# LayerNorm of all tokens beside the last expert unit, and a ring of 20 weight tiles, in a trunk layer with a hierarchical mixture of experts

## The chip, the cores and the metric

The kernel runs on one core of a Trainium2 chip. The metric is the device time of one execution in microseconds (us). The kernel before was timed in three runs.

## What is computed

One layer of a decoder trunk over 1024 tokens of width 1024, in float32. Token mixing (a Conformer convolution and a Mamba-2 scan side by side, and an output projection) ends in the first LayerNorm; each token then goes through two of 64 experts, and a second LayerNorm closes the layer. The change lies in the second half:

```python
x = layer_norm(DEEPNORM_ALPHA * x + g1 * mix, ln1_g[l], ln1_b[l])
h = x * (1.0 + sc2) + sh2
ffn = hier_moe(h, ...)              # each token: 2 experts of the 8 in its best group
x = layer_norm(DEEPNORM_ALPHA * x + g2 * ffn, ln2_g[l], ln2_b[l])
...
def expert_block(args):             # w1, w3: 1024 x 512, w2: 512 x 1024
    xb, e = args
    return (jax.nn.silu(xb @ w1[e]) * (xb @ w3[e])) @ w2[e]
```

## The kernel before, in words

Up to about 1080 us it does the token mixing; that part is the same in both kernels but for two instructions. Eight tiles of 128 tokens come out of the first LayerNorm; each is written to DRAM twice, as `x1d` (the normed token, L1003) and as `h2d` (modulated, what the experts read). The router's result is turned into tables of token numbers, gates and row numbers (`gidx`, `gslot`, `ridx`).

**The expert stage.** Every expert has six weight loads of 1 MB (w1, w3 and w2 in two halves each), so the plan has 64 x 6 = 384 loads. They go through a ring of 14 SBUF tiles (`N_RING`), all issued on the queue of SyncE (SP) by `load` (L244), in the order of the plan. A load is issued when the load that had its tile 14 places earlier has been used by every product that needs it (`emitted`). The first 13 (`N_EARLY`) are issued before the routing is known to the end, by a guess of the expert numbers (`fix_i`); the others follow the row `fix_l`, which is written behind the second gather.

Experts are ranked by their number of tokens, and 28 letters (`ORDER`) say how they are put together into units of at most 128 tokens: F and L are units of two experts, S of four, H of one, T is three units for two heavy experts (t4, t4x, t5 and so on; all three use the same weights). For experts of the small ranks the load is conditional: an expert without tokens is not read. The last unit is `s60`, the four smallest.

A unit (`unit`) gathers its tokens' rows from `h2d` into `xg` by an indirect DMA of GpSimd (POOL), transposes them on TensorE (`tp`), multiplies with w1 and w3 (`h0`, `h1`, L1325), takes Silu on ScalarE and the product on VectorE (`s1`), transposes (`th`), multiplies with w2 (`yp`, L1344), scales by the gate (L1349, VectorE) and scatters the rows into `ybuf` by another indirect DMA (L1283, POOL). `ybuf` has two rows per token, one for each of its experts. All the scatters write the same DRAM tensor and go one behind the other's landing.

**The end of before.** `load_sums` (L1270) reads `x1d` back into an SBUF tile `acc` of 4 MB at the start of the expert stage, and ScalarE multiplies it by alpha. `collect` (L1279, L1280) stands inside the last unit: 16 times it loads half of a tile's `ybuf` rows (0.5 MB, through two buffers `yb`) on POOL's queue and adds it into `acc` on VectorE. The last unit scatters nothing: its rows are split into a high and a low part and added by products with 0/1 matrices (`hots`, L1550) in `finish`, on top of `acc` (a product with the identity, L1541). `finish` then does the second LayerNorm tile by tile (L1551 to L1575) and stores on SP's queue (L1576). A loop for the tokens of overfull experts follows.

Of the kernel before, what the change touches and what calls it, by code (L numbers as in the profile page):

```python
# [19 lines left out]
P = 128  # L20
# [12 lines left out]
N_RING = 14  # L33
N_RING_A = 8
N_EARLY = 13
# [26 lines left out]
HW = 8  # L62
N_PRE = 3
# [7 lines left out]
FIN = "AV,VA,VA,VA,VA,VA,VA,VV".split(",")  # L71
# [24 lines left out]
ORDER = "FFSLSTLSHHLSTLSHHLSHHLHHSLLS"  # L96
# [5 lines left out]
def trunk(ctx: ExitStack, tc: tile.TileContext, x, c, w_ada, b_ada, w_in, conf_conv_w, conf_conv_b,  # L102
# [159 lines left out]
    with ExitStack() as p1:  # L262
# [64 lines left out]
        def ada_late(r, rows):  # L327
# [10 lines left out]
            else:  # L338
# [9 lines left out]
                nc.gpsimd.tensor_tensor(sc2_bc, sc2_bc, l1g_bc, op=OP.mult)  # L348

# [824 lines left out]
    with ExitStack() as p2:  # L1174
# [41 lines left out]
        rows = acc[:, 0, :].bitcast(BF16).rearrange("p (j t) -> p j t", t=P)  # L1216
# [42 lines left out]
    with ExitStack() as p3:  # L1259
# [8 lines left out]
        def load_sums():  # L1268
            for i in range(8):
                nc.scalar.dma_start(acc[:, i, :], x1d[i * P:(i + 1) * P, :])  # L1270
            for i in range(8):
                nc.scalar.activation(acc[:, i, :], acc[:, i, :], AF.Copy, scale=ALPHA)

        def collect():

            for i in range(8):
                for k in range(2):
                    yb = wk.tile([P, D], F32, tag="yb", bufs=2, name=f"yb{i}_{k}")
                    nc.gpsimd.dma_start(yb, ybuf[2 * i * P:2 * (i + 1) * P, :].rearrange("(t k) d -> t k d", k=2)[:, k, :])  # L1279
                    nc.vector.tensor_tensor(acc[:, i, :], acc[:, i, :], yb, op=OP.add)  # L1280

# [3 lines left out]
        load_sums()  # L1285
# [17 lines left out]
        def unit(nm, ws, cols, last=False):  # L1303
# [4 lines left out]
            if last:  # L1308
                collect()
# [20 lines left out]
            nc.scalar.activation(s1, hps[0], AF.Silu)  # L1330
            nc.vector.tensor_tensor(s1, s1, hps[1], op=OP.mult)  # L1331
# [18 lines left out]
            if not last:  # L1350
                send_rows(y, rcol)
                return

            trel = wk.tile([P, 8], F32, tag="trel", bufs=2, name=f"trel{nm}")
            nc.vector.tensor_scalar(trel, toff, -1.0, tcol, op0=OP.mult, op1=OP.add)
            hots = []
            for j in range(0, 8, HW):
                hot = wk.tile([P, HW, P], F32R, tag="hot", bufs=1, name=f"hot{nm}_{j}")
                nc.vector.tensor_tensor(hot, jf[:, None, :].to_broadcast([P, HW, P]),
                                        trel[:, j:j + HW, None].to_broadcast([P, HW, P]), op=OP.is_equal)  # L1360
                hots += [hot[:, i, :] for i in range(HW)]
            ys = []
            for n in range(2):
                yh, yl = (wk.tile([P, 512], F32R, tag=f"y{p_}", bufs=2, name=f"y{p_}{nm}_{n}") for p_ in "hl")
                nc.scalar.copy(yh, y[:, half[n]])
                nc.vector.tensor_tensor(yl, y[:, half[n]], yh, op=OP.subtract)
                ys.append((yh, yl))
            return hots, ys, y, rcol
# [95 lines left out]
        def emitted():  # L1464

            while sent[0] < len(plan):
                n = sent[0]
                if n >= N_RING and uses[n - N_RING] > 0:
                    break
                r, which, hf = plan[n]  # L1470
                if n >= min(N_RING, 6 * N_FIX):
                    load(ring[n % N_RING], *place_regs(r), which, hf)
# [11 lines left out]
        def tiles(r):  # L1484
            def of(which, hf):
# [3 lines left out]
                return ring[n % N_RING]  # L1489
# [30 lines left out]
        assert list(first.values()) == [P_TRI, P_HVY, P_LGT, P_SML, NE]  # L1520
        emitted()
# [6 lines left out]
        spare = [ring[(len(plan) + j) % N_RING] for j in range(N_RING)]  # L1528
        l2g_bc, l2b_bc = spare[0][:, 0:D], spare[0][:, D:2 * D]
        outs = [spare[1 + i // 2][:, D * (i % 2):D * (i % 2) + D] for i in range(8)]  # L1530
        banks = [("z", "z"), ("h0", "h1"), ("tp", "tp"), ("yp", "yp")] * 2

        def finish(nm, hots, ys, pre):

            zp = {}

            def z_open(i):
                zp[i] = [ps.tile([P, 512], F32, tag=banks[i][n], bufs=bufs_of[banks[i][n]], name=f"z{nm}{i}_{n}")
                         for n in range(2)]
                for n in range(2):  # L1540
                    nc.tensor.matmul(zp[i][n], ident, acc[:, i, half[n]], start=True, stop=not ys)  # L1541
            for i in range(pre):
                z_open(i)
            for i in range(8):
                if i >= pre:
                    z_open(i)
                bs = wk.tile([P, 2, 6], F32, tag="bs", bufs=4, name=f"bs{nm}{i}")
                for n in range(2):
                    for j in range(2 if ys else 0):
                        nc.tensor.matmul(zp[i][n], hots[i], ys[n][j], start=False, stop=(j == 1))  # L1550
                    nc.vector.bn_stats(bs[:, n, :], zp[i][n])  # L1551
                mv = wk.tile([P, 2], F32, tag="mv", bufs=4, name=f"mv{nm}{i}")
                nc.vector.bn_aggr(mv, bs)
                rs = wk.tile([P, 1], F32, tag="rs", bufs=4, name=f"rs{nm}{i}")
                nc.scalar.activation(rs, mv[:, 1:2], AF.Sqrt, bias=eps)
                nc.vector.reciprocal(rs, rs)
                t_ = outs[i]
                if "A" in FIN[i]:
                    nm_ = wk.tile([P, 1], F32, tag="nm", bufs=4, name=f"nm{nm}{i}")
                    nc.vector.scalar_tensor_tensor(nm_, mv[:, 0:1], -1.0, rs, op0=OP.mult, op1=OP.mult)  # L1560
                for n in range(2):
                    if FIN[i][n] == "V":

                        nc.vector.scalar_tensor_tensor(t_[:, half[n]], zp[i][n], mv[:, 0:1], l2g_bc[:, half[n]],
                                                       op0=OP.subtract, op1=OP.mult)
                    else:
# [61 lines left out]
```

## Time and profile before

| | |
|---|---|
| three runs | 2156.46, 2159.21, 2159.33 us |
| median | 2159.21 us |
| the profiled execution | 2157.99 us |
| its span, first to last instruction | 2156.0 us |
| mean granted TensorE clock | 0.94 |
| busy share of the span | TensorE 85%, VectorE 50%, GpSimd 29%, ScalarE 25% |
| expert stage | from about 1080 us to the end |

The profiled execution's own time lies 2.0 us above its span and 1.2 us below the median. The busy shares are means over the whole span: VectorE's 50% comes nearly all from the token mixing, and in the expert stage TensorE and the DMA engines carry the work.

### The profile page before, as it was taken

How to read it: one execution, taken by the hardware profiler on the slowest of the kernel's cores; microseconds unless marked ns; L12 is line 12 of the kernel's file. 1: busy time of each engine (PE TensorE's matmuls, PEld its weight loads, DVE VectorE, ACT ScalarE, POOL GpSimd, SP SyncE). 2: the span in 40 equal slices, each digit the busy share in tenths (PEclk: the TensorE clock that was granted, in tenths of full speed). 3: DMA queues.
4: the chain of work that ended last, by engine and by line, in shares of the span. 5: the costliest groups of instructions: out<-in, count | busy, mean ns of one | idle time of the engine just before them, and what ended most of it. 6: DMA issues, size and time to landing. Idle time of an engine off the chain costs nothing.

```text
span 2156.0 us, 23640 instructions
## 1 busy us (share of the span) xinstructions
PE 1826.5 (85%) x8135; PEld 1012.6 (47%) x8135; DVE 1073.0 (50%) x1796; ACT 547.7 (25%) x990; POOL 619.1 (29%) x440
## 2 busy tenths in 40 slices
PE   4897989689989999889678969989799897998784
PEld 1365656558667767767432313324234241433232
DVE  1499898977999999897830301000000000000036
ACT  0234535264344446443320000001000010000011
POOL 0345656651544346553510000100001000000014
PEclk7998999889989999999879999999999998999997
DMA  8877877646443425657489999899998999999964
GB/s 260 288 256 240 249 252 232 230 145 219 153 131 132 165 93 171 206 182 279 171 312 419 419 421 383 339 420 420 419 374 338 420 420 420 420 409 372 420 255 160
DMA packets 204278, 626.01 MB, mean 290 GB/s; under 512 B 25566, under 2 KB 91350, under 8 KB 157308
## 3 DMA queue, kind: packets, MB, share of 16 engines
q1 hardware_dynamic: 156080, 552.79, 66.9%
q10 hardware_dynamic: 36700, 46.51, 6.7%
q0 software_dynamic: 11376, 25.18, 3.3%
q8 instruction: 65, 1.06, 0.2%
q14 instruction: 57, 0.47, 0.1%
HBM read 576.08 MB, written 83.44 MB: 306 GB/s over the span
## 4 chain that ended last, share of the span: by engine, by line
PE 30%; DMA 26%; DVE 20%; issue 4%; ACT 2%; POOL 1%; ACTq 0%; SPq 0%; DVEq 0%; POOLq 0%
DMA ring<-in_expert_w_dram 24%; DVE acc L620 8%; PE mix L475 5%; PE h0h L1325 2%; PE h1h L1325 2%; PE ypl L1344 2%; PE yph L1344 2%; PE ypt L1344 1%; PE h1l L1325 1%; PE h0t L1325 1%; PE px L475 1%; PE h1t L1325 1%; PE h0l L1325 1%; DVE cy L694 1%; DVE ctl L950 1%
## 5 line engine op out<-in xcount | busy, mean ns | idle before, releaser
L620 DVE SCALAR_TENSOR_TENSOR acc<-u,cw,acc 128x512 f32<-128x512 f32 x426 | 433.3, 1029 | 17.5 <-ACT acc L609 13.5
L1290 POOL DMA_INDIRECT xg<-h2d,gidx x32 | 33.0, 1033 | 724.0 <-PE tph L1298 203.8
L475 PE MATMUL px<-hTh,wx_hl 128*128 128x512 f32 x512 | 175.3, 413 | 3.5 <-ACT wx_hl L448 3.0
L475 PE MATMUL mix<-wo_hl,cth 128*128 128x512 f32 x416 | 136.2, 421 | 14.9 <-DVE wo_hl L449 10.2
L1325 PE MATMUL h1s<-ring,xTs 128*32 128x512 f32 x512 | 99.3, 691 | 42.6 <-DMA ring<-in_expert_w_dram 42.6
L1344 PE MATMUL yps<-ring,hTs 128*32 128x512 f32 x512 | 109.5, 599 | 19.3 <-DMA ring<-in_expert_w_dram 16.9
L1331 DVE TENSOR_TENSOR s1s<-s1s,h1s 128x512 f32<-128x512 f32 x8 | 5.5, 688 | 223.2 <-PE h1s L1325 223.2
L475 PEld LDWEIGHTS px<-hTh,wx_hl 128*128 128x128 f32 x512 | 99.0, 195 | 36.0 <-ACT wx_hl L448 5.2
L475 PE MATMUL px<-hTl,wx_hl 128*128 128x512 f32 x256 | 105.1, 410 | 0.0
L475 PEld LDWEIGHTS mix<-wo_hl,cth 128*128 128x128 f32 x416 | 81.1, 199 | 38.4 <-DVE wo_hl L449 14.1
L449 POOL TENSOR_TENSOR wo_hl<-wo,wo_hl 128x512 fp32r<-128x512 f32 x52 | 76.1, 1473 | 60.5 <-ACT wo_hl L448 60.1
L305 PE MATMUL ada<-wada,cond 128*32 128x512 f32 x192 | 74.2, 673 | 21.9 <-DMA wada<-in_w_ada_dram 21.8
L475 PE MATMUL pg<-hTh,wg_hl 128*128 128x512 f32 x256 | 90.1, 419 | 1.9 <-ACT wg_hl L448 0.9
L1325 PE MATMUL h0s<-ring,xTs 128*32 128x512 f32 x512 | 75.6, 639 | 16.3 <-DMA ring<-in_expert_w_dram 16.3
L475 PE MATMUL pz<-hTh,wz_hl 128*128 128x512 f32 x256 | 86.2, 404 | 2.1 <-ACT wz_hl L448 1.1
L475 PE MATMUL mix<-wo_hl,ctl 128*128 128x512 f32 x208 | 80.3, 422 | 7.4 <-DVE ctl L950 7.3
L475 PE MATMUL pv<-hTh,wv_hl 128*128 128x512 f32 x256 | 85.7, 405 | 0.4 <-DVE h L514 0.4
L1325 PEld LDWEIGHTS h1s<-ring,xTs 128*32 128x32 f32 x512 | 22.0, 124 | 116.1 <-DMA ring<-in_expert_w_dram 75.3
L1349 DVE SCALAR_TENSOR_TENSOR ys<-yps,gslot,g_bc 128x512 f32<-128x512 f32 x16 | 12.0, 751 | 120.0 <-PE yps L1344 120.0
L448 ACT CAST wo_hl<-wo 128x512 fp32r<-128x512 f32 x104 | 63.1, 616 | 26.7 <-PE mix L475 14.7
L1344 PEld LDWEIGHTS yps<-ring,hTs 128*32 128x32 f32 x512 | 27.1, 109 | 87.5 <-issue 45.4
L1325 PE MATMUL h1l<-ring,xTl 128*64 128x512 f32 x256 | 63.1, 595 | 5.7 <-DMA ring<-in_expert_w_dram 5.7
(603 smaller groups left out, 3618.9 us busy)
## 6 DMA issues: line engine op xcount, KB each, us to landing
ring<-in_expert_w_dram SPq DMA_DIRECT2D x384, 1024.0 KB
wo<-in_w_out_dram SPq DMA_DIRECT2D x112, 256.0 KB
wada<-in_w_ada_dram SPq DMA_DIRECT2D x96, 256.0 KB
wind<-wx_hl SPq DMA_DIRECT2D x32, 512.0 KB
wx_hl<-wind SPq DMA_DIRECT2D x32, 512.0 KB
ybuf<-zeros ACTq DMA_DIRECT2D x8, 1024.0 KB
wind<-wg_hl SPq DMA_DIRECT2D x16, 512.0 KB
wind<-wv_hl SPq DMA_DIRECT2D x16, 512.0 KB
```

The source lines that it names most:

```text
L305: nc.tensor.matmul(pm[32 * j:32 * j + 32, :], lhs, wt, start=(k == 0), stop=(k == KT - 1), tile_position=(0, 32 * j))
L448: nc.scalar.copy(hi, wt)
L449: (eng or nc.gpsimd).tensor_tensor(lo, wt, hi, op=OP.subtract)
L475: nc.tensor.matmul(pt, lhs[a_], rhs[b_], start=(first and n == 0), stop=(last and n == 2))
L620: nc.vector.scalar_tensor_tensor(acc, u[:, j:j + HALF], cw[:, t, j:j + 1], acc, op0=OP.mult, op1=OP.add)
L694: nc.vector.scalar_tensor_tensor(acc, raw[:, j:j + HALF], sw[:, j, t:t + 1], acc, op0=OP.mult, op1=OP.add)
L950: nc.vector.tensor_tensor(cl, ck, ch, op=OP.subtract)
L1290: nc.gpsimd.indirect_dma_start(out=t_, out_offset=None, in_=h2d, in_offset=bass.IndirectOffsetOnAxis(ap=gcol, axis=0), bounds_check=T - 1, ...
L1325: nc.tensor.matmul(hp[a:b, :], xT[:, 4 * hf + k, a:b], w_[:, k, :], start=(hf + k == 0), stop=(hf + k == 4), tile_position=(0, a))
L1331: nc.vector.tensor_tensor(s1, s1, hps[1], op=OP.mult)
L1344: nc.tensor.matmul(yps[n][a:b, :], hT[:, 2 * hf + k, a:b], w_[:, k, 512 * n:512 * n + 512], start=(hf + k == 0), stop=(hf + k == 2), tile_ ...
L1349: nc.vector.scalar_tensor_tensor(y[:, half[n]], yps[n], gate, g2_bc[:, half[n]], op0=OP.mult, op1=OP.mult)
```

## The change

- **Ring.** `N_RING` goes from 14 to 20 and `N_EARLY` from 13 to 19. `acc`, `hot`, `yb`, `yh` and `yl` go, and the ring takes their place in SBUF. `x1d` is written already multiplied by alpha (two instructions on POOL, once, scale the LayerNorm's weight and bias).
- **Order of units.** The last four go from S L L S to L S L S, so the unit before the last is `l30` and the one before that `s56`.
- **Last loads.** The plan's last 24 loads (those of `s60`) turn in tiles 0 to 13 only. Tiles 14 to 19 (`back`), whose last weights are those of `l30`, then serve the end: two hold pairs of `ybuf` rows (1 MB), three hold six tiles z of `x1d` rows, one the second LayerNorm's weight and bias.
- **Sums.** `sums` does all eight tiles from DRAM: two loads on POOL's queue, two adds, the norm, and a store on POOL's queue. It counts only what is in `ybuf`, that is all units but the last.
- **Last unit.** `old_rows` then gathers the last unit's tokens once more from `x1d` and `ybuf`, adds them in PSUM, adds the last unit's result by a product with a matrix `same` (1 where two rows have the same token), norms these rows and scatters them over the output.
- **Order by hand.** The last unit's Silu, its product s1 and the first w2 product of its second half are kept in program order behind the sums.

```diff
-N_RING = 14
+N_RING = 20
-N_EARLY = 13
+N_EARLY = 19
+N_BACK = 6
...
-ORDER = "FFSLSTLSHHLSTLSHHLSHHLHHSLLS"
+ORDER = "FFSLSTLSHHLSTLSHHLSHHLHHLSLS"
...
+                nc.gpsimd.tensor_scalar(l1g_bc, l1g_bc, ALPHA, None, op0=OP.mult)
+                nc.gpsimd.tensor_scalar(l1b_bc, l1b_bc, ALPHA, None, op0=OP.mult)
...
-        def load_sums():
...
-        def collect():
...
             gcol, tcol, gate, rcol = cols
             xT = gather(gcol, nm)
-            if last:
-                collect()
+            if behind is not None:
+                behind()
...
+            pin = tc.keep_in_program_order if behind is not None else (lambda i_: i_)
+            pin(nc.scalar.activation(s1, hps[0], AF.Silu))
+            pin(nc.vector.tensor_tensor(s1, s1, hps[1], op=OP.mult))
...
+                            if hf and not n + k + a:
+                                pin(i_)
...
-                if n >= N_RING and uses[n - N_RING] > 0:
+                if prior[n] is not None and uses[prior[n]] > 0:
...
+        turn = (len(plan) - 24) // N_RING * N_RING
...
+            slots.append(n % N_RING if n < turn else (n - turn) % (N_RING - N_BACK))
...
-        def finish(nm, hots, ys, pre):
...
+        def sums(nm):
             for i in range(8):
...
+                z = singles[i % (len(singles) - 1)]
+                yy = pairs[i % 2]
+                nc.gpsimd.dma_start(z, x1d[i * P:(i + 1) * P, :])
+                nc.gpsimd.dma_start(yy, ybuf[2 * i * P:2 * (i + 1) * P, :].rearrange("(t k) d -> t k d", k=2))
+                for k in range(2):
+                    nc.vector.tensor_tensor(z, z, yy[:, k, :], op=OP.add)
+                mean, rs = norm([z[:, h_] for h_ in half], f"{nm}{i}")
+                nm_ = wk.tile([P, 1], F32, tag="nm", bufs=4, name=f"nm{nm}{i}")
+                nc.vector.scalar_tensor_tensor(nm_, mean, -1.0, rs, op0=OP.mult, op1=OP.mult)
+                nc.scalar.activation(z, z, AF.Identity, bias=nm_, scale=rs)
+                nc.vector.tensor_tensor(z, z, lng[:, 0], op=OP.mult)
+                nc.gpsimd.tensor_tensor(z, z, lng[:, 1], op=OP.add)
+                nc.gpsimd.dma_start(out[i * P:(i + 1) * P, :], z)
...
+        def old_rows():
+
+            sums("")
+            z = singles[-1]
+            yy = pairs[0]
+            for t_, src in ((z, x1d), (back[0], ybuf.rearrange("(t k) d -> t (k d)", k=2))):
+                nc.gpsimd.indirect_dma_start(out=t_, out_offset=None, in_=src,
+                                             in_offset=bass.IndirectOffsetOnAxis(ap=gcol, axis=0),
+                                             bounds_check=T - 1, oob_is_err=False)
+            sp = ps.tile([P, 512], F32, tag="tp", bufs=TPB, name="same_ps")
+            nc.tensor.matmul(sp[:, 0:P], tcol.to_broadcast([P, P]), ident, start=True, stop=True)
+            same = wk.tile([P, P], F32, bufs=1, name="same")
+            nc.vector.tensor_scalar(same, sp[:, 0:P], tcol, None, op0=OP.is_equal)
...
+                for j, t_ in enumerate((z, yy[:, 0], yy[:, 1])):
+                    nc.tensor.matmul(zp, ident, t_[:, half[n]], start=(j == 0), stop=False)
...
+        for n in range(2):
+            nc.tensor.matmul(zps[n], same, y_last[:, half[n]], start=False, stop=True)
+        mean, rs = norm(zps, "l")
...
+        nc.gpsimd.indirect_dma_start(out=out, out_offset=bass.IndirectOffsetOnAxis(ap=gcol, axis=0), in_=t_,
+                                     in_offset=None, bounds_check=T - 1, oob_is_err=False)
```

The scheduler that writes each engine's queue moves more than the diff says. Three places matter below.

**SP at the start of the expert stage.** Before, the five loads 8 to 12 (by `fix_i`; `ring_8683` to `ring_8687`) stood ahead of the two writes of `x1d`, and load 13 behind `fix_l`:

```order
L915 DMA wo_2_11_1_8436<-in_w_out_dram 128x512
L247 TENSOR_LOAD fix_i
L244 ISA
L244 DMA ring_8683<-in_expert_w_dram 128x2048
...
L244 DMA ring_8687<-in_expert_w_dram 128x2048
L1003 DMA x1d<-xr_8475 128x1024
L1003 DMA x1d<-xr_8477 128x1024
L247 TENSOR_LOAD fix_l
L244 ISA
L244 DMA ring_8688<-in_expert_w_dram 128x2048
```

Now, with lines moved by two or less in the first half:

```order
L915 DMA wo_2_11_1_8438<-in_w_out_dram 128x512
L1004 DMA x1d<-xr_8477 128x1024
L1004 DMA x1d<-xr_8479 128x1024
L245 TENSOR_LOAD fix_i
L242 ISA
L242 DMA ring_8682<-in_expert_w_dram 128x2048
...
L242 DMA ring_8692<-in_expert_w_dram 128x2048
L245 TENSOR_LOAD fix_l
L242 ISA
L242 DMA ring_8693<-in_expert_w_dram 128x2048
```

The two `x1d` writes stand ahead of eleven loads (8 to 18, `ring_8682` to `ring_8692`), and only load 19 stands behind `fix_l`.

**PE in the second T (t6, t6x, t7, then l22).** Before, the w2 products of t6x (`ypt6x`) followed its transpose `tht6x` at once. Now:

```order
L1320 MATMUL tht6x_10689<-ident_64,s1t6x_10686 128x128 x4
L1281 MATMUL tpt7_0_10738<-ident_64,xg0_8657 128x128 x4
L1281 MATMUL tpt7_1_10744<-ident_64,xg0_8657 128x128 x4
L1308 MATMUL h0t7_10750<-ring6_8133,xTt7_10737 128x512 x4
L1308 MATMUL h1t7_10773<-ring8_8682,xTt7_10737 128x512 x4
...
L1320 MATMUL tht7_10787<-ident_64,s1t7_10784 128x128 x4
...
L1308 MATMUL h0l22_10828<-ring12_8686,xTl22_10815 64x512
L1308 MATMUL h0l22_10828<-ring13_8687,xTl22_10815 64x512
```

All first products of t7, and the first half of l22's behind them, stand ahead of `ypt6x`, which reads t6's and t7's w2 tiles. The first T (t4, t4x, t5) keeps the order of before.

**POOL at the end.** Before, the scatters of s56, l28 and l30 stood ahead of the `yb` loads. Now (`ring16` to `ring18` are the z tiles, `ring14` and `ring15` the pairs; each z tile's half has a row):

```order
L1267 DMA ybuf_90<-yl28_11982,ridx_8664 2048x1024
L1534 DMA ring16_8690<-x1d_86 128x1024
L1534 DMA ring17_8691<-x1d_86 128x1024
...
L1534 DMA ring18_8692<-x1d_86 128x1024
L1556 DMA ring18_8692<-x1d_86,gidx_8663 128x1024
L1267 DMA ybuf_90<-ys56_12168,ridx_8664 2048x1024
L1267 DMA ybuf_90<-yl30_12258,ridx_8664 2048x1024
L1535 DMA ring14_8688<-ybuf_90 128x2048
L1535 DMA ring15_8689<-ybuf_90 128x2048
```

Five z loads and a gather (six rows, into the tiles that l30's w2 products read last) stand ahead of the scatter of s56, then that of l30, then the loads of the pairs.

## Rows read from the trace of the kernel before

**Rows 1.** Stretches of 40 us: engines' busy us, PEclk, DMA share, GB/s.

```profile
1120.00:1160.00 40.00, 37.11 (x196) 13.80 (x198) 3.69 (x5) 3.92 (x7) 4.06 (x4) 1.00 1.01 420
...
1320.00:1360.00 40.00, 38.87 (x149) 16.32 (x149) 3.69 (x5) 3.44 (x6) 4.06 (x4) 1.00 0.83 306
1360.00:1400.00 40.00, 37.74 (x187) 15.37 (x189) 4.38 (x6) 3.91 (x7) 4.05 (x4) 1.00 0.95 376
...
1600.00:1640.00 40.00, 37.74 (x135) 16.53 (x132) 3.63 (x5) 3.93 (x7) 2.03 (x2) 1.00 0.77 281
...
1920.00:1960.00 40.00, 37.37 (x102) 17.04 (x101) 3.44 (x5) 4.09 (x8) 4.07 (x4) 1.00 0.93 364
```

**Rows 2.** What SP waited for, 1080 to 2064 us: total, times, longest.

```profile
SPq L244 <- PE h0t6x L1325: 18.1, 2, 13.5
SPq L244 <- PE h0t4x L1325: 17.8, 2, 12.4
```

**Rows 3.** SP's own issues around 1080 us, from the timeline.

```profile
1050.14 5.49 SPq L244 DMA_DIRECT2D ring<-in_expert_w_dram  x5
1078.69 2.69 SPq L1003 DMA_DIRECT2D x1d<-xr  x2
1101.78 27.93 SPq L244 DMA_DIRECT2D ring<-in_expert_w_dram  x13
```

**Rows 4.** Stretches of 10 us at the stage's start, columns as in rows 1.

```profile
1100.00:1110.00 10.00, 8.93 (x34) 3.89 (x36) 0.31 (x2) 2.46 (x3) 0.99 (x1) 0.69 0.52 167
1110.00:1120.00 10.00, 9.15 (x44) 3.88 (x41) 0.69 (x1) 0.60 (x1) 0.00 (x0) 1.00 0.94 366
```

**Rows 5.** Timeline from the end of l30: POOL, then DVE.

```profile
2063.81 0.97 POOL L1283 DMA_INDIRECT ybuf<-yl,ridx  x1 [31.15 <-DVE yl L1349]
2069.60 1.15 POOL L1279 DMA_DIRECT2D yb<-ybuf  x2 [4.82 <-DMA ybuf<-yl,ridx]
...
2076.75 0.69 DVE L1331 TENSOR_TENSOR s1s<-s1s,h1s 128x512 f32<-128x512 f32 x1 [13.22 <-PE h1s L1325]
2085.94 1.22 DVE L1280 TENSOR_TENSOR acc<-acc,yb 128x1024 f32<-128x1024 f32 x1
2087.07 0.74 DVE L1349 SCALAR_TENSOR_TENSOR ys<-yps,gslot,g_bc 128x512 f32<-128x512 f32 x1
2140.79 1.30 DVE L1551 BATCH_NORM_STATS2 bs<-z 128x6 f32<-128x512 f32 x2 [1.65 <-PE z L1550]
2143.88 1.28 DVE L1572 SCALAR_TENSOR_TENSOR ring<-ring,rs,ring 128x1024 f32<-128x1024 f32 x1
```

**Rows 6.** DMA issues, 1000 to 2156 us: KB each, median us to landing.

```profile
yb<-ybuf POOLq DMA_DIRECT2D x16, 512.0 KB, 4.4
...
ybuf<-yl,ridx POOLq DMA_INDIRECT x8, 8.8
```

**Rows 7.** Groups by form, 2086 to 2146 us: busy us, mean ns, idle before.

```profile
L1280 DVE TENSOR_TENSOR acc<-acc,yb 128x1024 f32<-128x1024 f32 x15 | 22.0, 1465 | 4.7 <-DMA yb<-ybuf 4.7
L1551 DVE BATCH_NORM_STATS2 bs<-z 128x6 f32<-128x512 f32 x16 | 10.6, 688 | 3.8 <-PE z L1550 3.8
L1560 DVE SCALAR_TENSOR_TENSOR nm<-mv,rs 128x1 f32<-128x1 f32 x7 | 2.5, 354 | 0.2
L1553 DVE BATCH_NORM_AGGREGATE mv<-bs 128x2 f32<-128x12 f32 x8 | 1.6, 204 | 0.2
L1555 ACT ACT_TABLE_LOAD x1 | 1.3, 1283 | 0.0
```

**Rows 8.** POOL's part of the second LayerNorm in the timeline, 2100 to 2104 us.

```profile
2100.28 1.26 POOL L1574 TENSOR_TENSOR ring<-ring,ring 128x512 f32<-128x512 f32 x1
2101.62 2.15 POOL L1575 TENSOR_TENSOR ring<-ring,ring 128x512 f32<-128x512 f32 x1
```

**Rows 9.** PE after a pause and 25 us later: first products of two units.

```profile
1102.94 5.30 PE L1325 MATMUL h0f<-ring,xTf 128*64 128x512 f32 x16
...
1128.58 3.65 PE L1325 MATMUL h0f<-ring,xTf 128*64 128x512 f32 x16
```

More of the change, by code (lines that the diff above doesn't have):

```diff
@@ L1349, in unit @@
                 nc.vector.scalar_tensor_tensor(y[:, half[n]], yps[n], gate, g2_bc[:, half[n]], op0=OP.mult, op1=OP.mult)
[L1350 to L1368, printed above, removed]
+            if last:
+                return y
+            send_rows(y, rcol)
         def overflow_tables():
@@ L1471, in emitted @@
                 if n >= min(N_RING, 6 * N_FIX):
-                    load(ring[n % N_RING], *place_regs(r), which, hf)
+                    load(ring[slots[n]], *place_regs(r), which, hf)
                 sent[0] += 1
@@ L1520, in trunk @@
         assert list(first.values()) == [P_TRI, P_HVY, P_LGT, P_SML, NE]
+        turn = (len(plan) - 24) // N_RING * N_RING
+        held = {}
+        for n in range(len(plan)):
+            slots.append(n % N_RING if n < turn else (n - turn) % (N_RING - N_BACK))
+            prior.append(held.get(slots[n]))
+            held[slots[n]] = n
+        back = [ring[N_RING - N_BACK + j] for j in range(N_BACK)]
         emitted()
@@ L1525, in trunk @@
             unit(nm, [tiles(r) for r in places], cols_of(u))
[L1528 to L1531, printed above, removed]
-        def finish(nm, hots, ys, pre):
[L1535 to L1543, printed above, removed]
-            for i in range(8):
[L1545 to L1566, printed above, removed]
-                        nc.scalar.activation(t_[:, half[n]], zp[i][n], AF.Identity, bias=nm_, scale=rs)
-                for k in "VA":
-                    if k in FIN[i]:
-                        s_ = slice(0, D) if FIN[i] == k + k else half[FIN[i].index(k)]
-                        if k == "V":
-                            nc.vector.scalar_tensor_tensor(t_[:, s_], t_[:, s_], rs, l2b_bc[:, s_], op0=OP.mult, op1=OP.add)
-                        else:
-                            nc.gpsimd.tensor_tensor(t_[:, s_], t_[:, s_], l2g_bc[:, s_], op=OP.mult)
-                            nc.gpsimd.tensor_tensor(t_[:, s_], t_[:, s_], l2b_bc[:, s_], op=OP.add)
-                nc.sync.dma_start(out[i * P:(i + 1) * P, :], t_)
@@ new lines, in trunk, with norm @@
+        singles = [back[2 + j // 2][:, D * (j % 2):D * (j % 2) + D] for j in range(6)]
+        def norm(z, nm):
+            bs = wk.tile([P, 2, 6], F32, tag="bs", bufs=4, name=f"bs{nm}")
+            for n in range(2):
+                nc.vector.bn_stats(bs[:, n, :], z[n])
+            mv = wk.tile([P, 2], F32, tag="mv", bufs=4, name=f"mv{nm}")
+            nc.vector.bn_aggr(mv, bs)
+            rs = wk.tile([P, 1], F32, tag="rs", bufs=4, name=f"rs{nm}")
+            nc.scalar.activation(rs, mv[:, 1:2], AF.Sqrt, bias=eps)
+            nc.vector.reciprocal(rs, rs)
+            return mv[:, 0:1], rs
@@ new lines, in trunk @@
+        y_last = unit(nm, [tiles(r) for r in places], cols_of(u), True, old_rows)
+        assert not any(uses.values())
+        same = zps.pop()
+        for n in range(2):
+            nc.tensor.matmul(zps[n], same, y_last[:, half[n]], start=False, stop=True)
+        mean, rs = norm(zps, "l")
+        t_ = wk.tile([P, D], F32, tag="y", bufs=2, name="tl")
+        for n in range(2):
+            nc.vector.scalar_tensor_tensor(t_[:, half[n]], zps[n], mean, lng[:, 0, half[n]], op0=OP.subtract, op1=OP.mult)
+            nc.vector.scalar_tensor_tensor(t_[:, half[n]], t_[:, half[n]], rs, lng[:, 1, half[n]], op0=OP.mult, op1=OP.add)
```

53 lines of the change are left out of this document (21 added, 32 removed).

## Prediction

> **What bounds the kernel now.** I read the profile from the end backwards. The table of 40 us stretches comes first: at the expert stage's full pace the DMA engines move 420 GB/s, so a 1 MB load takes 2.5 us, and a stretch below that is time in which the weight stream stood [rows 1]. 306 and 376 GB/s in the first T come to (420 - 306) / 420 x 40 = 10.9 and 4.2 us, 281 in the second T to 13.2, 364 in the run of H units to 5.3. The stretches beside these, by the same working, add 1.4 and 1.8 us to the second and 1.8 to the third. TensorE is busy for 37 to 39 of the 40 us there: the ring is full, and SP waits for products to give tiles back. The chain says the same from the other side: outside these places it runs along the loads, and SP's waits name the products, with one of 12.4 us behind t4x and one of 13.5 us behind t6x [rows 2]. Then comes the timeline of the end: l30's scatter is issued at 2063.81, and the span ends at 2156.0, 92.2 us later [rows 5]. No load is left to wait for there; it is a chain of reads, adds and norms. So the change works on two things: the weight stream, and that tail. The sum is made against the profiled execution, 2157.99 us, 1.2 below the median.
>
> **The start of the stream.** Before, loads 8 to 12 went out at 1050.14, the two `x1d` writes at 1078.69, and load 13 only at 1101.78, behind `fix_l` [rows 3]. In the 20 us after 1100 the rates are 167 and 366 GB/s, that is 1.67 + 3.66 = 5.3 MB with some 0.6 MB of gathers in it, four and a half loads, so 17.5 have landed by 1120 [rows 4]. Now the writes stand ahead of eleven loads, so eight loads lie in the ring until about 1081.4, and from there nothing holds the queue up to load 19. To 1120 that is 38.6 us x 420 GB/s = 16.2 MB, less 3 MB of `x1d` and `h2d` writes and gathers, 12.5 loads: 20.5 landed instead of 17.5. The freed 4 MB read of `acc` is what lets them through. **Three loads ahead: -7.5 us.** Bounds 0 (the writes come later, or the ring waits for the first unit) and -12.
>
> **The T and H stretches.** Six more tiles hold 6 x 2.5 = 15 us of loads ahead of TensorE. In the first T, where the order of products stays, the longest wait of 12.4 us [rows 2] fits into that; waits of 2 to 3 us for single tiles stay: **-12 us** of 15.1, bounds -6 and -15. In the second T the order that was shown takes it back: t6x's w2 products now come behind t7's first products and l22's first half, so the tiles they hold come free a unit later, and the deeper ring is filled all the same. I take **0** of the 16.4 us there and 0 of the 7.1 us at the H units, where units are interleaved too; bounds 0 and -23. Units before the last change places (S L L S to L S L S), but the same loads stand ahead of l30's last product: 0.
>
> **The tail, from l30's rows ready to the end, 92.2 us before.** POOL's queue is the new path:
>
> - Five z loads and a gather wait for l30's last w2 product. At 0.55 us an issue (a pair took 1.15 [rows 5]) and 1.0 for the gather, 3.7 us from that product, which lies 1 us ahead of the start: 2.7.
> - Behind them, s56's scatter, long ready. A scatter in this stage takes 8.8 us to land [rows 6], and 5.8 where little else ran (2063.81 to 2069.60 [rows 5]). It shares the engines with 2.5 MB of z: 8.8.
> - l30's scatter waits for that landing: 5.8.
> - The first pair: 4.4 us for 0.5 MB [rows 6] and 1.2 for the other half, 5.6.
>
> So the first add comes at 22.9, bounds 18 and 29. I read a page beside this: by the Trainium skill, DMA: Bandwidth & Descriptors, section on the anatomy of one DMA on the GpSimd path, such a transfer takes about 2.0 us and its bytes over 436 GB/s. That would be 4.4 for the pair, an estimate, and the sum 1.2 us shorter; the measured half is already above the page's 3.2, so the row decides.
>
> A step of `sums` costs VectorE two adds and a product of 1024 columns, two bn_stats, one bn_aggr, the reciprocal and the small product: 3 x 1.465 + 2 x 0.688 + 0.2 + 0.2 + 0.35 = 6.5 us [rows 7], with the adds at their mean beside POOL's work. Eight steps are **52 us**, and 2 more because a z tile is loaded again only when its store has landed. Pairs (two buffers, 5.6 us) and ScalarE keep up. From below: adds alone at 1.22 [rows 5], 5.8 a step, 46; from above 66 (the third rival).
>
> Then the last unit, behind the last Identity (1.5 us ahead of the last step's end). Table load and Silu 1.9 [rows 7]; from s1 to the end of its rows 2076.75 to 2087.81, 11.1 [rows 5]; the product with `same` 1.0; a norm as for the last tile before, 2140.79 to 2145.16, 4.4 [rows 5]. TensorE has stood, and its first products after a pause took 5.30 us at a granted clock of 0.69 where 3.65 is usual [rows 9, 4]: 1.7 more. That is 20.1. The scatter into the output 5.8, and from the last landing to the span's end about 8.5: the last store was issued at the end of the last instruction, 2145.16, and the span ended 10.8 later, some 2 us of it the store's own.
>
> 22.9 + 54 - 1.5 + 20.1 + 5.8 + 8.5 = **109.8, 17.6 more than 92.2**; bounds +6 and +31. What hid the last unit before goes: its products ran beside the first `ybuf` loads; of it only h0, h1 and the gather run beside the sums now. The two extra instructions on POOL in the first half, the `same` matrix and the second LayerNorm's weights (loaded on ScalarE's queue while the scatters land) are off every path: 0. The `yh`, `yl` and `hots` work and 16 rounds of products that are removed lay on the tail and are gone with the 92.2.
>
> **The sum.** -7.5 - 12 + 17.6 = -1.9: 2156.1 us for the profiled execution, 2157.3 beside the median. About 0.2% (4.3 us) is what a measurement of this kernel can tell from no change, so this is no change.
>
> **Rivals.**
>
> 1. *No change, as summed.* Range 2150 to 2165. For it: both terms are of one size, and each rests on queues that are written down. Chance 0.36.
>
> 2. *The ring wins.* Its depth clears the later stretches too, though t6x's tiles come late: a wait there needs the stream to be a full ring ahead, and the longer lookahead meets it half-way. 8 of the 23 us would do: 2149; all, with the scatters landing in 5.8 each, 2131. For it: TensorE has slack of several us in every 40 outside those stretches [rows 1]. Against: the tile order. Chance 0.33.
>
> 3. *The adds and POOL's additions exclude each other: slower.* POOL's instruction took 2.15 us beside VectorE's and 1.26 without [rows 8], and VectorE's adds 1.465 in the mean, so each waits for the other. If they exclude each other fully, every step pays POOL's 1024 columns, 2 x 1.26 = 2.5, on top of VectorE's own 5.8: 8.3 us, 66 for eight, 14 more than summed: 2171. It decides from 7.3 us a step on (6 us more over eight steps). The Trainium skill, SBUF — State Buffer, section on the two separate sides, calls the port that VectorE and GpSimd share an exclusive lock, held for a whole instruction; the rows above agree. Against: half of VectorE's step is in instructions that did not grow. Chance 0.2.
>
> 4. *The stream does not start earlier, and the first T keeps half its stall*: the ring then gives 6 instead of 19.5, 2171. Chance 0.11.
>
> **Numbers.** Forecast 2157.5. The range must take in rival 2 up to about ten more us won and rivals 3 and 4: 2143 to 2173. Faster by over 0.2%: 0.34; within: 0.36; slower: 0.30.
>
> **What would show it.** Right: after 1081 the stream runs at 420 GB/s without the gap to 1102; the first T at over 400 GB/s, the second still near 300; l30's rows ready about 19 us earlier (2044); on POOL z loads, then two scatters one behind the other's landing, the first add some 23 us after; eight steps of 6 to 7 us; then some 20 us with one unit's small work, TensorE at half its clock at first. Wrong: a second T without stall (rival 2); steps of over 7.3 us with POOL and VectorE alternating (rival 3); a first T still at 306 GB/s (rival 4); or a first add within 15 us of l30's end, which would void my chain of scatters.

## The result, and the profile after

The changed kernel took 2173.82 us (median of 4 runs, 2172.23 to 2175.76), the kernel before beside it 2159.04: a ratio of 1.0078, 95% interval 1.0065 to 1.009. It is 15 us slower by the two medians (17 by the ratio), where no change was forecast, and the time lies just above the range.

Three marks cut both profiles into three parts: the issue of the last two `x1d` writes on SP (the end of the token mixing), the end of VectorE's scaling of l30's rows, and the end of the span. By these marks:

| part, us | before | after | difference | forecast |
|---|---|---|---|---|
| token mixing, to the `x1d` writes | 1078.7 | 1088.1 | +9.4 | 0 |
| weight stream, writes to l30's rows | 984.8 | 967.9 | -16.9 | -19.5 |
| tail, l30's rows to the end | 92.5 | 117.5 | +25.0 | +17.6 |
| span | 2156.0 | 2173.5 | +17.5 | -1.9 |

SP's issues in the timeline of the changed kernel show the first mark, and the load stream behind it:

```profile
1088.06 2.68 SPq L1004 DMA_DIRECT2D x1d<-xr  x2
1091.38 55.37 SPq L242 DMA_DIRECT2D ring<-in_expert_w_dram  x26
```

Beside [rows 3] the writes are 9.4 us later. The loads follow 3.3 us behind them. SP still waits twice before load 19, 6.3 us for a write of `h2d` and 9.8 us for `fix_l`, but enough loads are in flight: the rate is 317 GB/s from 1090 to 1100 and 426 and 420 in the two stretches of 10 us behind it. So the stream has no gap, as forecast, and it is late only because the mixing is. The 40 us stretches, columns as in [rows 1]:

```profile
1320.00:1360.00 40.00, 38.87 (x150) 16.43 (x149) 3.69 (x5) 2.84 (x5) 3.02 (x3) 1.00 1.01 418
1360.00:1400.00 40.00, 37.73 (x171) 15.97 (x171) 2.70 (x4) 4.52 (x8) 3.03 (x3) 1.00 0.98 392
...
1600.00:1640.00 40.00, 37.90 (x147) 16.99 (x148) 3.69 (x6) 4.61 (x8) 5.01 (x5) 1.00 0.61 233
1920.00:1960.00 40.00, 36.83 (x133) 15.60 (x132) 4.02 (x6) 4.07 (x7) 2.29 (x3) 1.00 0.92 371
```

The first T went from 306 and 376 GB/s to 418 and 392: by the same working, with 412 in the stretch behind, its stall is 3.6 us instead of 15.1. The second T, 281 before, is at 233: with the stretch behind, 18.2 us instead of 16.4. The H units keep 6.5 of 7.1.

The tail, POOL's timeline, and behind it two rows of VectorE's:

```profile
2055.39 1.06 POOL L1556 DMA_INDIRECT ring<-x1d,gidx  x1 [1.17 <-PE ypl L1329]
2056.76 1.04 POOL L1267 DMA_INDIRECT ybuf<-ys,ridx  x1 [0.30 <-issue]
2074.64 0.99 POOL L1267 DMA_INDIRECT ybuf<-yl,ridx  x1 [16.84 <-DMA ybuf<-ys,ridx]
2077.69 1.14 POOL L1535 DMA_DIRECT2D ring<-ybuf  x2 [2.06 <-DMA ybuf<-yl,ridx]
...
2082.82 2.48 DVE L1537 TENSOR_TENSOR ring<-ring,ring 128x1024 f32<-128x1024 f32 x2 [26.85 <-DMA ring<-ybuf]
2141.88 0.69 DVE L1316 TENSOR_TENSOR s1s<-s1s,h1s 128x512 f32<-128x512 f32 x1 [0.68 <-ACT s1s L1315]
```

l30's rows were ready at 2055.96. s56's scatter, ready since 2023.55, goes out behind the z loads at 2056.76 and holds the next for 17.9 us; the first add comes 26.9 us after l30's rows, and the last unit's s1 only behind the sums.

### The profile page after: what moved, and what is told of

It reads as the page before. It is cut to its first block, busy times and chain, and to the rows that moved or that the text cites. A ratio compares the mean times of both kernels' runs of the same rounds, so it can differ in the third digit from the quotient of the medians.

```text
span 2173.5 us, 23420 instructions
## 1 busy us (share of the span) xinstructions
PE 1808.8 (83%) x8089; PEld 1004.0 (46%) x8089; DVE 1065.7 (49%) x1793; ACT 547.4 (25%) x984; POOL 623.7 (29%) x446
## 5 line engine op out<-in xcount | busy, mean ns | idle before, releaser
L620 DVE SCALAR_TENSOR_TENSOR acc<-u,cw,acc 128x512 f32<-128x512 f32 x426 | 426.0, 1013 | 20.4 <-ACT acc L609 11.2
L1329 PE MATMUL yps<-ring,hTs 128*32 128x512 f32 x512 | 110.8, 610 | 18.6 <-DMA ring<-in_expert_w_dram 16.3
L1308 PE MATMUL h1s<-ring,xTs 128*32 128x512 f32 x512 | 94.0, 678 | 36.2 <-DMA ring<-in_expert_w_dram 36.1
L475 PEld LDWEIGHTS mix<-wo_hl,cth 128*128 128x128 f32 x416 | 80.9, 199 | 39.6 <-DVE wo_hl L449 13.1
L1316 DVE TENSOR_TENSOR s1h<-s1h,h1h 128x512 f32<-128x512 f32 x8 | 5.5, 687 | 170.0 <-PE h1h L1308 170.0
L733 POOL TENSOR_TENSOR dec<-ab,future 128x512 f32<-128x512 f32 x32 | 48.0, 1502 | 89.6 <-DMA ab<-acsd 49.7
L1316 DVE TENSOR_TENSOR s1l<-s1l,h1l 128x512 f32<-128x512 f32 x8 | 5.5, 687 | 135.7 <-PE h1l L1308 135.7
```

Of the source, the lines that this page charges most:

```text
L475: nc.tensor.matmul(pt, lhs[a_], rhs[b_], start=(first and n == 0), stop=(last and n == 2))
L620: nc.vector.scalar_tensor_tensor(acc, u[:, j:j + HALF], cw[:, t, j:j + 1], acc, op0=OP.mult, op1=OP.add)
L733: nc.gpsimd.tensor_tensor(dec, ab, future[:, None, :].to_broadcast([P, 4, P]), op=OP.add)
L1308: nc.tensor.matmul(hp[a:b, :], xT[:, 4 * hf + k, a:b], w_[:, k, :], start=(hf + k == 0), stop=(hf + k == 4), tile_position=(0, a))
L1316: pin(nc.vector.tensor_tensor(s1, s1, hps[1], op=OP.mult))
L1329: i_ = nc.tensor.matmul(yps[n][a:b, :], hT[:, 2 * hf + k, a:b], w_[:, k, 512 * n:512 * n + 512], start=(hf + k == 0), stop=(hf + k == 2), ...
```

## The experiments

All runs are timed against the kernel before on the same chip; where the parts are given, they are by the three marks, each from one profile.

| run | median us | ratio, 95% interval | mixing | stream | tail |
|---|---|---|---|---|---|
| alpha in the sums | 2161.39 | 1.0014 (1.0004 to 1.0024) | 1079.4 | 967.8 | 112.4 |
| before, with the two instructions | 2164.82 | 1.003 (1.002 to 1.0041) | 1083.6 | 985.1 | 92.5 |
| scatters first | 2169.23 | 1.0059 (1.0039 to 1.008) | 1084.2 | 968.4 | 113.3 |
| t7 in turn | 2160.58 | 1.0014 (1.0004 to 1.0024) | 1087.3 | 957.1 | 117.8 |
| sums split | 2160.60 | 1.0015 (1.0003 to 1.0027) | 1086.8 | 968.7 | 106.1 |
| norm on VectorE | 2165.05 | 1.004 (1.0023 to 1.0057) | 1084.4 | 967.4 | 110.1 |
| all in turn | 2162.28 | 1.0021 (1.0008 to 1.0034) | 1085.4 | 956.8 | 117.1 |
| combined | 2132.99 | 0.989 (0.9866 to 0.9914) | 1078.7 | 956.7 | 97.5 |
| the two instructions later | 2173.85 | 1.0085 (1.0067 to 1.0103) | 1085.5 | 968.2 | 116.8 |
| combined, pair first | 2126.01 | 0.9857 (0.984 to 0.9873) | 1079.6 | 957.1 | 89.9 |

The parts say more than the medians here. The mixing alone ended anywhere from 1083.6 to 1088.1 in the eight profiles that have the two POOL instructions, and from 1078.7 to 1079.6 in the four that have not, so a difference of 4 us in a median may be the mixing's.

### The token mixing: the two POOL instructions

The mixing follows the kernel before to within 1 us until 400 us. There POOL's timeline in the changed kernel shows the two new instructions, between the splits of the weights that TensorE takes (`_hl`, a high and a low part):

```profile
403.82 3.10 POOL L348 TENSOR_SCALAR l1b_bc<-l1b_bc 128x1024 f32<-128x1024 f32 x1
...
410.57 2.96 POOL L449 TENSOR_TENSOR wx_hl<-wx,wx_hl 128x512 fp32r<-128x512 f32 x2
413.51 3.21 POOL L347 TENSOR_SCALAR l1g_bc<-l1g_bc 128x1024 f32<-128x1024 f32 x1
416.69 1.29 POOL L449 TENSOR_TENSOR wx_hl<-wx,wx_hl 128x512 fp32r<-128x512 f32 x1
```

The first half has the same instructions in both kernels but for these two, yet behind them its queues stand in another order. That is a fourth place where the scheduler moved things, beside the three named with the change. POOL's queue, in the kernel before and then in the changed one:

```profile
421.26 1.86 POOL L616 TENSOR_TENSOR tap<-tap,tap 128x512 f32<-128x512 f32 x1 [5.13 <-DVE xd L760]
423.09 1.73 POOL L733 TENSOR_TENSOR dec<-ab,future 128x512 f32<-128x512 f32 x1
424.78 1.75 POOL L449 TENSOR_TENSOR wz_hl<-wz,wz_hl 128x512 fp32r<-128x512 f32 x1
```

```profile
420.92 1.27 POOL L733 TENSOR_TENSOR dec<-ab,future 128x512 f32<-128x512 f32 x1 [2.94 <-PE y L755]
422.14 1.28 POOL L449 TENSOR_TENSOR wz_hl<-wz,wz_hl 128x512 fp32r<-128x512 f32 x1
423.38 1.71 POOL L616 TENSOR_TENSOR tap<-tap,tap 128x512 f32<-128x512 f32 x1
```

Compared row by row in the traces, from 400 to 900 us some 450 of VectorE's 1500 rows of the first half stand elsewhere. So the two instructions bring two things at once, their own time and a new order.

**Alpha in the sums** (`e1_alpha_in_sums`):

```diff
-                nc.gpsimd.tensor_scalar(l1g_bc, l1g_bc, ALPHA, None, op0=OP.mult)
-                nc.gpsimd.tensor_scalar(l1b_bc, l1b_bc, ALPHA, None, op0=OP.mult)
...
-                for k in range(2):
-                    nc.vector.tensor_tensor(z, z, yy[:, k, :], op=OP.add)
+                nc.vector.scalar_tensor_tensor(z, z, ALPHA, yy[:, 0, :], op0=OP.mult, op1=OP.add)
+                nc.vector.tensor_tensor(z, z, yy[:, 1, :], op=OP.add)
```

(and the rows gathered for the last unit are scaled once on ScalarE.)

> 

> The changed kernel without the two POOL instructions that scale the LayerNorm weights by alpha; alpha goes into the first add of each step of the sums instead (same instruction count). Theory A (these two instructions, at 404 to 417 us, cost the token mixing its 9.4 us): the last x1d writes are issued near 1079 instead of 1088, the loads start near 1082 instead of 1091.4, l30's rows are ready near 2046.5 instead of 2056, the time is about 2164.5 (2162 to 2167). Rival B (the mixing is late for another reason, as the SBUF places or the larger ring): the writes stay near 1088 and the time near 2174.

**The kernel before, with the two instructions** (`e2_before_with_ops`): the two lines are added after L348 of before, and ScalarE's pass over `acc` multiplies by 1.

> 

> The kernel before, with the two POOL instructions alone (x1d written times alpha; ScalarE's pass over acc then multiplies by 1). Theory A: the mixing ends 9 us later here too, the whole expert stage shifts with it, 2168 (2165 to 2171). Rival B (they cost nothing by themselves): 2159.

SP's timeline, the first kernel and then the second:

```profile
1079.35 2.68 SPq L1002 DMA_DIRECT2D x1d<-xr  x2
1082.66 47.66 SPq L242 DMA_DIRECT2D ring<-in_expert_w_dram  x22
```

```profile
1055.04 5.49 SPq L244 DMA_DIRECT2D ring<-in_expert_w_dram  x5
1083.60 2.69 SPq L1005 DMA_DIRECT2D x1d<-xr  x2
1106.95 17.55 SPq L244 DMA_DIRECT2D ring<-in_expert_w_dram  x9
```

Without the two instructions the writes are back at 1079.35, the stream unchanged at 967.8, the time 12 us lower: theory A by the writes. (5.2 of the 12 are the tail's: ScalarE's scaling stands behind the sums in the code, and in this run the last unit's Silu went ahead of the sums, at 2062.87, so that run has two effects.) Added alone to the kernel before, they move its writes by 4.9 us, and its median by 7.1 (0.3%), less than theory A's 9. So adding the two instructions causes the mixing's delay: 5 us in the old kernel, 8.7 between the run without them and the changed one. The orders go with them: without them the queues are in the order of before, and the kernel before with the two has the order of the changed kernel.

**The two instructions later** (`e9_ops_later`): the same two, kept some 500 us later on POOL's queue, ahead of the first product of an `x1d` tile.

> 

> The changed kernel with the same two POOL instructions kept some 450 us later on POOL's queue, ahead of the first x1d rows, where the order of the first half is else that of the kernel before. Theory A (their place at 404 to 417 us costs: POOL's splits of the weights come later there, and the scheduler put the queues behind them in another order): the last x1d writes near 1079 to 1082, time 2164 to 2168. Rival B (6 us more on POOL cost the mixing its 5 to 9 us wherever they stand): writes at 1084 to 1088, 2171 to 2175.

```profile
1085.52 2.81 SPq L1007 DMA_DIRECT2D x1d<-xr  x2
```

The writes came at 1085.52, the time stayed at 2173.85: rival B by both numbers, so their place at 404 us is not what costs. This is not a clean second place, though: they also held the first product of an `x1d` tile back, from 896 us before to 919, and from about 900 us on the queues are again in another order. Up to there the run stays within some 2 us of the kernel before; the delay begins where the two instructions stand. What is shown is that adding them, in two places, costs the mixing 5 to 9 us. Whether their 6.3 us on POOL or the order that the scheduler writes around them costs the time is open: no run has the one without the other.

### The second T: the order of TensorE's products

**t7 in turn** (`e4_t7_in_turn`): the first products of t7 and l22 are queued behind the last w2 product of the unit before (`last_yp`); `IN_TURN` holds the two names.

```diff
-                            nc.tensor.matmul(hp[a:b, :], xT[:, 4 * hf + k, a:b], w_[:, k, :], start=(hf + k == 0),
-                                             stop=(hf + k == 4), tile_position=(0, a))
+                            with tc.issue_after(last_yp[0].ins) if nm in IN_TURN else nullcontext():
+                                nc.tensor.matmul(hp[a:b, :], xT[:, 4 * hf + k, a:b], w_[:, k, :],
+                                                 start=(hf + k == 0), stop=(hf + k == 4), tile_position=(0, a))
```

> 

> The changed kernel with the products of t7 and l22 kept behind the w2 products of the unit before them, as in the kernel before. Theory A (the second T keeps its stall because t6x's w2 products come late): the stall there falls from 18 us (233 GB/s in 1600 to 1640) to 4 to 7, as in the first T, l30's rows are ready some 12 us earlier, time 2161 to 2164. Rival B (20 tiles are not enough there whatever the order, or the gain is lost at the H units): stall 12 us or more there, or the H units' 6.5 us grow by as much; time 2170 or more.

What SP waited for on t6x's w2 products (total, times, longest), in the changed kernel and then with t7 in turn, and the two stretches of the latter:

```profile
SPq L242 <- PE ypt6x L1329: 31.0, 2, 28.8
```

```profile
SPq L243 <- PE ypt6x L1332: 6.8, 2, 6.4
```

```profile
1600.00:1640.00 40.00, 38.58 (x138) 16.50 (x137) 4.30 (x7) 3.91 (x7) 6.04 (x6) 1.00 0.97 376
1920.00:1960.00 40.00, 37.55 (x161) 14.89 (x161) 5.52 (x8) 4.01 (x7) 4.04 (x4) 1.00 0.88 343
```

The wait of 28.8 us is 6.4, the stall of that stretch 4.2 us instead of 17.8, and the stream 10.8 us shorter: theory A. The stretch of the H units went from 371 GB/s to 343, less than rival B's price. So the order took the second T's gain, and 20 tiles are enough for both.

**All in turn** (`e7_all_in_turn`): the same for every unit.

> 

> As the run with t7 in turn, for every unit: its first products stay behind the w2 products of the unit before. Theory A (the interleaving costs the H units too: 371 GB/s in 1920 to 1960, 6.5 us in all): that stretch goes to 410 or more, 2155 to 2158. Rival B (the H units' stall is there in either order): 2159 to 2162, like the run with t7 alone.

```profile
1920.00:1960.00 40.00, 37.70 (x149) 15.00 (x147) 4.95 (x7) 3.93 (x7) 2.03 (x2) 1.00 1.01 408
```

The H stretch rose to 408 GB/s, but the stream (956.8) and the time did not follow: rival B by the time, against its reason, since the stall did go with the order. In the stretch from 2000 to 2040 the rate is 328 GB/s, where the run with t7 alone has 401, and SP waits there for next to no product: the weights came in earlier, but l30's rows, counted from the `x1d` writes, did not. What held these was not tried.

### The tail: the scatter, the sums, the last unit

**Scatters first** (`e3_scatter_first`): `with tc.issue_after(<l30's scatter>)` around the z loads and the gather from `x1d`.

> 

> The changed kernel with one order changed: the z loads and the gather from x1d stand on POOL's queue behind l30's scatter, so s56's scatter goes out when its rows are ready (about 2024) and not after l30. Theory A (the wait for two scatters one behind the other, 26.9 us from l30's rows to the first add, comes from that place in the queue): the first add 14 to 16 us after l30's rows, time about 2162 (2160 to 2165). Rival B (the scatter is slow because of what else moves then, whichever scatter it is): l30's scatter now takes 15 us or more, the first add 22 us or more after, time 2170 or more.

POOL's timeline of that run, and the first add:

```profile
2052.86 0.97 POOL L1267 DMA_INDIRECT ybuf<-yl,ridx  x1 [32.09 <-DVE yl L1339]
2053.83 2.74 POOL L1537 DMA_DIRECT2D ring<-x1d  x5
2056.87 1.07 POOL L1560 DMA_INDIRECT ring<-x1d,gidx  x1 [0.30 <-issue]
2061.68 1.07 POOL L1538 DMA_DIRECT2D ring<-ybuf  x2 [3.74 <-DMA ybuf<-yl,ridx]
...
2075.28 2.49 DVE L1540 TENSOR_TENSOR ring<-ring,ring 128x1024 f32<-128x1024 f32 x2 [22.70 <-DMA ring<-ybuf]
```

s56's scatter goes out early and l30's 0.3 us after its rows, and lands in 8.8 us. But the first pair then takes 13.6 us, where it took 5.1 in the changed kernel: the first add comes at 22.7 instead of 26.9. Neither theory: the order is worth 4 us, and the rest moves from the scatter to the load. Whichever stands behind the z loads on POOL's queue lands late, in a stretch full of transfers. The DMA issues of the changed kernel from 2040 to 2090 us (median us to landing last):

```profile
ring<-ybuf POOLq DMA_DIRECT2D x4, 1024.0 KB, 5.1
ring<-x1d POOLq DMA_DIRECT2D x5, 512.0 KB, 12.7
...
ybuf<-ys,ridx POOLq DMA_INDIRECT x1, 17.1
ybuf<-yl,ridx POOLq DMA_INDIRECT x1, 2.8
```

From 2046 to 2074 SP's queue moves 5.4 MB, the last weights, POOL's 2.7 MB, nearly all z, and ScalarE's 1 MB of norm weights. s56's scatter among them takes 17.1 us. l30's, with 63 GB/s in all from 2075 to 2080, takes 2.8, and 8.5 in the run above.

**Sums split** (`e5_split_sums`): steps 0 to 2 stand ahead of the last unit's second half, steps 3 to 7 and the gather behind it (`N_FIRST` is 3).

```diff
-            sums("")
+            sums("", range(0, N_FIRST))
+
+        def add_old():
+
+            sums("", range(N_FIRST, 8))
             z = singles[-1]
```

> 

> The changed kernel with the last unit's second half (Silu, s1, w2 products) traced and kept behind step 3 of the sums instead of step 8; the other five steps, then the gather and the rest follow. Theory A (of the 33 us from the last step's Identity to the end some 11, s1 to y, are there only because of the order, and fit beside the sums): from the last step's Identity to the end 20 to 23 us, time 2162 to 2166. Rival B (VectorE then waits for TensorE inside the sums and loses the same): sums 66 us or more, time 2171 to 2174.

```profile
2108.34 0.60 ACT L1316 ACTIVATE s1s<-h0s 128x512 f32<-128x512 f32 x1
```

The Silu ran at 2108.34 in the middle of the sums, and the tail took 106.1 us instead of 117.5: theory A, with a miss. From the last step's Identity to the end it is 25.1 us where 33.6 were and 20 to 23 were expected; the other 3.4 us came from the sums, 55.0 instead of 58.4, for which theory A had no reason. In all 11 us went with the order.

**The norm on VectorE** (`e6_norm_on_vector`):

```diff
-                nm_ = wk.tile([P, 1], F32, tag="nm", bufs=4, name=f"nm{nm}{i}")
-                nc.vector.scalar_tensor_tensor(nm_, mean, -1.0, rs, op0=OP.mult, op1=OP.mult)
-                nc.scalar.activation(z, z, AF.Identity, bias=nm_, scale=rs)
-                nc.vector.tensor_tensor(z, z, lng[:, 0], op=OP.mult)
-                nc.gpsimd.tensor_tensor(z, z, lng[:, 1], op=OP.add)
+                nc.vector.scalar_tensor_tensor(z, z, mean, lng[:, 0], op0=OP.subtract, op1=OP.mult)
+                nc.vector.scalar_tensor_tensor(z, z, rs, lng[:, 1], op0=OP.mult, op1=OP.add)
```

> 

> The changed kernel with the end of each step on VectorE alone: two scalar_tensor_tensor of 1024 columns in place of ScalarE's Identity, VectorE's product and POOL's addition. VectorE's own work grows from 5.5 to 6.6 us a step. Theory A (VectorE and POOL keep each other waiting: some 12 of the 58.4 us from the first add to the last step's end): 52 to 55 us for that stretch, time 2168 to 2171. Rival B (the steps wait for pairs and z tiles): 58 us or more, time 2173 or more.

VectorE's groups over the sums (busy us, mean ns), in the changed kernel and then in this run:

```profile
L1537 DVE TENSOR_TENSOR ring<-ring,ring 128x1024 f32<-128x1024 f32 x16 | 21.0, 1319 | 29.0 <-DMA ring<-ybuf 27.2 <-DMA ring<-x1d 1.7
L1542 DVE TENSOR_TENSOR ring<-ring,ring 128x1024 f32<-128x1024 f32 x8 | 11.8, 1472 | 3.7 <-ACT ring L1541 3.7
L1540 DVE SCALAR_TENSOR_TENSOR nm<-mv,rs 128x1 f32<-128x1 f32 x8 | 9.6, 1206 | 0.1
```

```profile
L1537 DVE TENSOR_TENSOR ring<-ring,ring 128x1024 f32<-128x1024 f32 x16 | 19.2, 1203 | 28.9 <-DMA ring<-ybuf 28.8
L1539 DVE SCALAR_TENSOR_TENSOR ring<-ring,mv,ring 128x1024 f32<-128x1024 f32 x8 | 10.2, 1279 | 0.0
L1540 DVE SCALAR_TENSOR_TENSOR ring<-ring,rs,ring 128x1024 f32<-128x1024 f32 x8 | 10.2, 1278 | 0.0
```

With POOL's additions gone the adds take 1.20 us each instead of 1.32, and the sums 53.4 us instead of 58.4, although VectorE issues more columns: theory A by the stretch. The edit takes out ScalarE's pass as well, for which VectorE had stood 3.7 us; the groups shown fall from 42.4 busy us to 39.6. So the 5.0 us are not POOL's additions alone. The tail is 7.4 us shorter; the median came out 3 us below the expectation, where the mixing of this profile was 3.7 earlier too. The small product nm, one column wide, had taken 1.2 us in the mean. In four of the eight steps it took 0.11 to 0.15 us, in the other four 2.2 to 2.3, and there it ended when an addition of POOL did:

```profile
2090.24 0.14 DVE L1540 SCALAR_TENSOR_TENSOR nm<-mv,rs 128x1 f32<-128x1 f32 x1
2118.97 2.33 POOL L1543 TENSOR_TENSOR ring<-ring,ring 128x1024 f32<-128x1024 f32 x1 [0.55 <-DVE rs L1526]
2118.99 2.33 DVE L1540 SCALAR_TENSOR_TENSOR nm<-mv,rs 128x1 f32<-128x1 f32 x1
```

### Together

**Combined** (`e8_combined`): alpha in the sums, scatters first, all in turn, sums split, norm on VectorE; the products that add the last unit's old rows are also kept behind its w2 products.

> 

> All of these together: alpha in the sums, scatters ahead of the z loads, every unit in turn, the last unit's second half behind step 3, the norm on VectorE. Theory A (the terms are separate and add): -9 (mixing) - 12 (second T) - 4 (scatter) - 9 (last unit) - 4 (norm) from 2173.8: 2136 (2130 to 2142), below the kernel before. Rival B (an earlier stream and earlier scatters run into the last unit's weights, so half of the tail's gain is lost): 2143 to 2150.

2132.99 us: theory A, and 3 us below its sum. By the marks the mixing gives 9.4 us, the stream 11.2 and the tail 20.0; the three tail runs by themselves gave 4.2, 11.4 and 7.4, 23.0 in all, so there a little is lost. It is 1.1% faster than the kernel before.

**Combined, pair first** (`e10_pair_first`): POOL's queue takes z 0, pair 0, z 1, pair 1, and only then the other three z loads and the gather.

> 

> The combined kernel with the first two pairs of ybuf rows ahead of z tiles 2 to 4 and of the gather on POOL's queue. Theory A (the first pair, issued 10.7 us after l30's rows, lands late because 2.5 MB of z stand ahead of it on the same queue): the first add 15 to 19 us after l30's rows instead of 23.7, time 2126 to 2130. Rival B (it lands late because all transfers share the engines, the last unit's weights above all): first add 21 us or more after, time 2131 to 2135.

```profile
2046.06 1.09 POOL L1540 DMA_DIRECT2D ring<-ybuf  x2 [5.38 <-DMA ybuf<-yl,ridx]
```

```profile
2036.94 0.97 POOL L1267 DMA_INDIRECT ybuf<-yl,ridx  x1 [31.44 <-DVE yl L1341]
2037.90 0.62 POOL L1539 DMA_DIRECT2D ring<-x1d  x1
2047.62 0.56 POOL L1540 DMA_DIRECT2D ring<-ybuf  x1 [9.10 <-issue]
...
2055.68 1.23 DVE L1543 SCALAR_TENSOR_TENSOR ring<-ring,ring 128x1024 f32<-128x1024 f32 x1 [19.01 <-DMA ring<-ybuf]
```

The first row is the combined kernel's, where the first add came at 2059.01; the others are this run's. The pair lands 8.1 us after its issue instead of 12.9, and the first add comes 19.0 us after l30's rows instead of 23.7: theory A at the end of its range. The sums behind it took 51.7 us instead of 55.5, which neither theory had. 2126.01 us, 1.4% faster than the kernel before (ratio 0.9857, 0.984 to 0.9873) and the best of all; its tail of 89.9 us is shorter than the old one's 92.5.

## Why the prediction was wrong

The directions held: a shorter stream and a longer tail. But the two came to +8.1 us where -1.9 was forecast, and 9.4 us came from a part that was set to nothing. By the marks the span missed the forecast by 19.4 us: 9.4 in the mixing, 2.6 in the stream and 7.4 in the tail. Every term that was given bounds for its size came out within them but that of the second T and the H units (+1.2 in all, bounds 0 and -23); the zero for the two instructions had none.

- **"The two extra instructions on POOL in the first half ... are off every path: 0."** This is the step that failed. Adding them moved the end of the mixing by 9.4 us in the changed kernel's profile, and by 5 to 9 in the eight profiles that have them: about half of the miss. I named no work that hides them, and the bounds left them out. In the trace POOL's row around 400 us stood between splits of weights for TensorE, and its 29% of the span is a mean over two halves, the first of them busy. With them came another order of the first half's queues, which the forecast did not look at; which of the two costs is open. With the 8.7 us of the run without them taken off, the change would come to some 2165 us, an estimate: inside the range, yet 0.3% slower where no change was forecast.
- **The start of the stream, -7.5.** Right by itself: of the -16.9 us, 11.4 are the first T's, and -1.8 and 0.6 the second T's and the H units', so -6.7 is left for the start, counted from the `x1d` writes. It is a rest and was not measured by itself.
- **The first T, -12, and 0 at the second T.** Right: -11.4 and +1.8, and the reason for the second, t6x's late w2 products, is shown by the run with t7 in turn. Rival 2 is out: depth alone does not clear that stall (18.2 us), nor did the order alone with 14 tiles (16.4); both together leave 4.2.
- **The scatters, 22.9 to the first add.** 26.9. The chain was the one described, but s56's scatter took 17.9 us from issue to release where I took 8.8, and l30's 3.05 where I took 5.8. The median of a stage at its steady pace was no price for a scatter behind five z loads on its own queue and beside the last weights. Nor was 5.8 the price "where little else ran": from 2064 to 2070 the DMA engines moved 274 GB/s in the kernel before, and with little else l30's scatter took 2.8. The first pair took 5.1, and 5.6 was forecast. By the Trainium skill, DMA: Bandwidth & Descriptors, section on the anatomy of one DMA, it would be 4.4, an estimate; the row lies between.
- **The sums, 54.** 58.4, a term sized too small: 7.3 us a step, the very mark from which the prediction let rival 3 decide. Its mechanism is at work, at a part of its price: the sums came 4.4 us above the forecast where full exclusion was to cost 12, and 5.0 us went with POOL's additions and ScalarE's pass together. By the Trainium skill, SBUF — State Buffer, section on the two separate sides, an instruction of VectorE with two inputs in SBUF and one of GpSimd that reads SBUF shut each other out of the port they share, each for its whole length. The trace agrees: the one-column product took 1.2 us in the mean, against 0.35 before [rows 7], and up to 2.33 beside one of POOL's additions.
- **The last unit, 18.6 behind the sums' end, and 14.3 to the end of the span.** 17.9 and 14.4: right. That it need not stand there is what the split sums show.
- **Rival 4**: the stream did start later in time, but for the mixing and not for the queue, and the first T lost most of its stall: out.

## What to carry to other kernels

Ask of every instruction that a change adds, however far from its subject, which engine's queue it lengthens and what that queue feeds there; a mean busy share over the span says nothing about that place. Compare the order of all queues before and after over the whole kernel, not only near the change. Price a transfer from a stretch that is as full as the one it will run in, and look at what stands ahead of it on its own queue. A deeper ring buys only as much as the order of the products lets its tiles come free.

## What was unexpected of the hardware

Adding two instructions of 6.3 us to POOL cost the mixing 5 to 9 us in all eight profiles that have them, in two different places; as the order of the queues changed with them, this is shown of the kernel and not of the engine. An indirect scatter of one unit landed in 17.1 us behind the z loads, and that of the next in 2.8 us with little else moving. And a VectorE instruction of one column took up to 2.33 us beside POOL's additions of 1024 columns and 0.14 without, so that a cheap instruction became as dear as a wide one.
